# First attention of a two-block transformer: values in column halves, scores four pairs ahead, output weights by contraction tile

## The chip, the cores and the metric

One core of a Trainium2 chip runs the whole program in one launch. The metric is device time in microseconds (us). Engines: TensorE (PE) multiplies 128x128 stationary tiles with moving tiles; VectorE (DVE), ScalarE (ACT) and GpSimd (POOL) work element by element; DMA queues bring weights from memory. Products land in PSUM, in eight banks of 128 partitions by 512 floats. Each engine works through its own queue in order.

## The reference

256 tokens of 1024 features go through two blocks in float32. Block 1 is a gated-linear-attention layer (GLA), an MLP, the sliding-window attention that is edited here, and a second MLP. Block 2 is a mixer of two attentions with gates, an MLP and a gated embedding product. The edited attention, cut to what is computed:

```python
q = (h @ w_q).reshape(B, NB, BLOCK, SWA_KV_HEADS, SWA_GROUP, SWA_HEAD_DIM)   # 16 heads of 64, 2 key heads
s = einsum('bnqhgd,bnkhd->bnhgqk', q, kb) * SWA_HEAD_DIM ** -0.5             # blocks of 128 queries, 256 keys
s = where(mask, s + bias, NEG)
m = maximum(max(s, -1), sink)
p = exp(s - m)
p = p / (sum(p, -1) + exp(sink - m))
o = einsum('bnhgqk,bnkhd->bnqhgd', p, vb)
x = x + o.reshape(B, T, 1024) @ w_out
```

## The kernel before

Activations are kept transposed, features on partitions and the 256 tokens along the free axis. Every float32 weight tile is split on the chip into a high and a low part, so that one product becomes three matmuls (high by high, high by low, low by high; `mmA`, lines 271 to 276). Weights come in chunks of 1 MB (128 x 2048) by DMA; `Weights.pump` (line 64) splits half a chunk: a CAST on ACT (`wh`, L80) and a subtraction on DVE (`wl`, L81). `take` hands out the next chunk. A pump stands after each piece of matmul work, and the order of the written code is the order in each engine's queue; nothing reorders it.

`pair` multiplies one chunk, which is two outputs of 128 features over all eight contraction tiles, and yields in the middle, so that other work can be put between its halves (`Fill`). `late_two` does the same for two chunks whose input is still being made, with the last contraction tiles last.

The attention works on eight pairs of heads, f = 0 to 7. For each: `swa_scores` (S: four matmuls, then on DVE bias and maximum, L851, and small operations to L857; on ACT four exponentials, L864, in place in `s`), `swa_T` (six transposes of `s`, copied to `pt` by ACT, L874), `swa_values` (O: `pt` is stationary, and the values `vs` with a column of ones move, so that column 64 is the row sum; DVE adds the sink's term, takes the reciprocal and multiplies into `ot`, L887 to L890), `swa_oT` (OT: transposes of `ot`, split to `oT_h` by ACT and `oT_l` by DVE, L904 and L905), `swa_out` (the pair's share of the output product, for the first four outputs). Scores run two pairs ahead; the projection's third and fourth chunk (q of outputs 4 to 7) fill the first rounds. Outputs 4 to 7 are two whole chunks, `o12` and `o13`, at the end, with the residual additions (`residual`, L388, and L371, L376 for the next MLP's input `xs`) between them. Then the MLP's first product, named m1u, begins with the first six contraction tiles of four outputs.

`Banks` gives out the eight banks of PSUM in the order in which they came free. The same scheme of residuals, with all eight outputs by contraction tile, stands at the end of the GLA layer (`oa`), ahead of the MLP product m0u.

## Time and profile before

| | us |
|---|---|
| median of three runs (lowest, highest) | 1015.9 (1014.09, 1018.38) |
| profiled execution, and its span | 1012.64, 1010.9 |
| PE busy | 987.6 (98%) |
| PE weight loads | 887.5 (88%) |
| DVE busy | 656.3 (65%) |
| ACT busy | 572.6 (57%) |
| POOL busy | 214.1 (21%) |
| the stage that is edited, 328.46 to 392.03 | 63.57 |

Busy time is a share over stages with different limits. The start of a matmul is recorded, its end is modelled, so durations of successive matmuls overlap, and the distance of two starts tells the pace. A number in brackets at a line's end is the idle time of that engine ahead of it, with what ended it.

### The profile page before, as it was taken

How to read it: one execution, taken by the hardware profiler on the slowest of the kernel's cores; microseconds unless marked ns; L12 is line 12 of the kernel's file. 1: busy time of each engine (PE TensorE's matmuls, PEld its weight loads, DVE VectorE, ACT ScalarE, POOL GpSimd, SP SyncE). 2: the span in 40 equal slices, each digit the busy share in tenths (PEclk: the TensorE clock that was granted, in tenths of full speed). 3: DMA queues.
4: the chain of work that ended last, by engine and by line, in shares of the span. 5: the costliest groups of instructions: out<-in, count | busy, mean ns of one | idle time of the engine just before them, and what ended most of it. 6: DMA issues, size and time to landing. Idle time of an engine off the chain costs nothing.

```text
span 1010.9 us, 16329 instructions
## 1 busy us (share of the span) xinstructions
PE 987.6 (98%) x6540; PEld 887.5 (88%) x6540; DVE 656.3 (65%) x996; ACT 572.6 (57%) x983; POOL 214.1 (21%) x244
## 2 busy tenths in 40 slices
PE   7999999999999999999999999998999999999996
PEld 6879988888889889888888889898999988888896
DVE  5856678875555766787555537776466688755555
ACT  5734458874344665787454444365555588744343
POOL 3203123330001002333011216202212233300001
PEclk9999999999999999999999999999999999999998
DMA  7543535655557214565555633635355456555521
GB/s 265 180 165 128 181 115 204 219 197 193 195 196 239 95 62 145 190 233 205 200 175 178 221 125 123 220 114 171 121 187 189 167 173 243 174 201 190 195 84 42
DMA packets 26395, 174.47 MB, mean 173 GB/s; under 512 B 3284, under 2 KB 3576, under 8 KB 6224
## 3 DMA queue, kind: packets, MB, share of 16 engines
q1 hardware_dynamic: 24336, 168.11, 47.9%
q0 software_dynamic: 1696, 5.21, 1.8%
q8 instruction: 51, 0.84, 0.3%
q14 instruction: 24, 0.20, 0.1%
q10 hardware_dynamic: 288, 0.12, 0.0%
HBM read 172.32 MB, written 1.11 MB: 172 GB/s over the span
## 4 chain that ended last, share of the span: by engine, by line
PE 82%; DVE 8%; issue 4%; ACT 3%; POOL 2%; DMA 0%; POOLq 0%; DVEq 0%; ACTq 0%
PE m2u L280 6%; PE m1d L280 6%; PE m1u L280 6%; PE m2d L280 6%; PE m0d L280 6%; PE m0u L280 6%; PE m1u L281 3%; PE m2u L281 3%; PE m0d L281 3%; PE m2d L281 3%; PE m1d L281 3%; PE m0u L281 3%; DVE wl L81 2%; PE g L274 1%; PE g L276 1%
## 5 line engine op out<-in xcount | busy, mean ns | idle before, releaser
L81 DVE TENSOR_TENSOR wl<-raw,wh 128x1024 fp32r<-128x1024 f32 x316 | 387.6, 1248 | 126.4 <-ACT wh L80 121.0
L80 ACT CAST wh<-raw 128x1024 fp32r<-128x1024 f32 x316 | 321.6, 1047 | 84.5 <-issue 41.4
L230 POOL TENSOR_TENSOR acc<-acc,sq 128x256 f32<-128x256 f32 x52 | 39.5, 765 | 362.8 <-ACT sq L229 362.1
L720 POOL TENSOR_TENSOR us<-s,us 128x256 fp32r<-128x256 f32 x96 | 81.4, 848 | 161.9 <-ACT us L719 161.9
L280 PE MATMUL m0u<-xs,wh 128*128 128x512 f32 x256 | 89.7, 396 | 0.9 <-DVE xs L376 0.9
L280 PE MATMUL m2u<-xs,wh 128*128 128x512 f32 x256 | 89.2, 395 | 0.0
L280 PE MATMUL m1u<-xs,wh 128*128 128x512 f32 x256 | 89.1, 394 | 0.0
L280 PE MATMUL m0d<-us,wh 128*128 128x512 f32 x256 | 88.8, 394 | 0.0
L280 PE MATMUL m1d<-us,wh 128*128 128x512 f32 x256 | 88.8, 394 | 0.0
L280 PE MATMUL m2d<-us,wh 128*128 128x512 f32 x256 | 88.8, 394 | 0.0
L371 ACT ACTIVATE xs<-x,gains 128x256 fp32r<-128x256 f32 x40 | 19.0, 504 | 94.7 <-DVE x L770 72.7
L281 PE MATMUL m0u<-xs,wl 128*128 128x256 f32 x256 | 71.0, 277 | 0.0
L281 PE MATMUL m2u<-xs,wl 128*128 128x256 f32 x256 | 71.0, 277 | 0.0
L281 PE MATMUL m1u<-xs,wl 128*128 128x256 f32 x256 | 71.0, 277 | 0.0
L281 PE MATMUL m0d<-us,wl 128*128 128x256 f32 x256 | 70.9, 277 | 0.0
L281 PE MATMUL m2d<-us,wl 128*128 128x256 f32 x256 | 70.9, 277 | 0.0
L281 PE MATMUL m1d<-us,wl 128*128 128x256 f32 x256 | 70.9, 277 | 0.0
L280 PEld LDWEIGHTS m0u<-xs,wh 128*128 128x128 f32 x256 | 48.0, 188 | 12.8 <-DVE xs L376 1.8
L280 PEld LDWEIGHTS m1d<-us,wh 128*128 128x128 f32 x256 | 48.0, 188 | 11.1
L280 PEld LDWEIGHTS m2d<-us,wh 128*128 128x128 f32 x256 | 48.0, 188 | 11.1
L280 PEld LDWEIGHTS m2u<-xs,wh 128*128 128x128 f32 x256 | 48.0, 188 | 11.1
L280 PEld LDWEIGHTS m0d<-us,wh 128*128 128x128 f32 x256 | 48.0, 188 | 11.1
(387 smaller groups left out, 2503.8 us busy)
## 6 DMA issues: line engine op xcount, KB each, us to landing
raw<-in_w_up SPq DMA_DIRECT2D x48, 1024.0 KB, 4.8
raw<-in_w_dn SPq DMA_DIRECT2D x48, 1024.0 KB, 4.8
raw<-in_w_oa SPq DMA_DIRECT2D x8, 1024.0 KB, 4.8
raw<-in_w_g SPq DMA_DIRECT2D x8, 1024.0 KB, 5.0
raw<-in_w_o SPq DMA_DIRECT2D x6, 1024.0 KB, 5.0
raw<-in_w_v SPq DMA_DIRECT2D x4, 1024.0 KB, 5.6
raw<-in_w_gate SPq DMA_DIRECT2D x4, 1024.0 KB, 4.8
raw<-in_w_q SPq DMA_DIRECT2D x4, 1024.0 KB, 4.9
```

Of the source, the lines that this page charges most:

```text
L80: nc.scalar.copy(h[:, sl], t[:, sl])
L81: nc.vector.tensor_tensor(l[:, sl], t[:, sl], h[:, sl].bitcast(F32), ALU.subtract)
L230: eng.tensor_tensor(acc, acc, sq, ALU.add)
L274: mm(ps, wh, xh, start=first, stop=False, skip_group_check=True)
L276: mm(ps, wl, xh, start=False, stop=last, skip_group_check=True)
L280: mm(ps, w[0], xs[2][:, k].rearrange("p s t -> p (s t)"), start=first, stop=False, skip_group_check=True)
L281: mm(ps[:, :T], w[1], xs[0][:, k, :], start=False, stop=last, skip_group_check=True)
L371: nc.scalar.activation(self.xs[0][:, k, :], x[:, k, :], AF.Copy, scale=self.gain(k))
L720: nc.gpsimd.tensor_tensor(us[1][:, o, :], s, us[0][:, o, :].bitcast(F32), ALU.subtract)
```

## The change

The change is in this one attention, and in what orders its weights.

- Weights come as q0, keys and values, q1, q2, q3, then the output weights packed in four chunks of two contraction tiles by eight outputs. `late_two` works on q0 and keys/values together; q1 is third.
- In the stage the subtraction `wl` of a pump is held back until the next pump or `take` (`W.lag`, `settle`). Pumps stand only in every second round.
- Scores run four pairs ahead, with five buffers `s`; the exponentials also sum their rows (`accum_out`). `swa_divide` divides `s` before the transposes: on DVE, from the third pair on the second head's half on GpSimd.
- `swa_values` has `vs` (64 columns, no ones) as the stationary tile and `pt` moving, for the two heads in two column halves of the array; its output is already transposed, so `ot` and `swa_oT` are gone.
- `swa_out` adds a pair's share to all eight outputs, in four banks, from the third round on. The products `o12` and `o13` at the end are gone; residuals follow each second output of the last pair.

The diff, without three hunks of set-up and with long removed blocks cut:

```diff
@@ -77,8 +78,11 @@
...
             sl = slice(q * CH // 2, (q + 1) * CH // 2)
+            self.settle()
             nc.scalar.copy(h[:, sl], t[:, sl])
-            nc.vector.tensor_tensor(l[:, sl], t[:, sl], h[:, sl].bitcast(F32), ALU.subtract)
+            self.owed = lambda e=self.low: e.tensor_tensor(l[:, sl], t[:, sl], h[:, sl].bitcast(F32), ALU.subtract)
+            if not self.lag:
+                self.settle()
             self.part = (h, l, t, 1)
@@ -86,10 +90,18 @@
...
+    def settle(self):
+        if self.owed:
+            self.owed()
+            self.owed = None
     def take(self):
...
             self.pump()
+        if i == self.n_split - 1:
+            self.settle()
         self.cur += 1
@@ -158,8 +170,7 @@
...
     add("w_up0"), add("w_dn0")
-    add("w_q1", [0, 1]), add("w_kv"), add("w_q1", [2, 3])
-    add("w_o1k"), add("w_o1")
+    add("w_q1", [0]), add("w_kv"), add("w_q1", [1, 2, 3]), add("w_o1")
     add("w_up1"), add("w_dn1")
@@ -293,36 +305,36 @@
...
-    def pair(xs, name, evac, own=False):
+    def pair(xs, name, evac, own=False, pumps=(1, 2)):
...
         pair_part(ps, w, xs, 0, range(NK))
-        W.pump()
+        W.pump(pumps[0])
         yield
...
             B.done(ps)
-        W.pump(2)
+        W.pump(pumps[1])
         yield
-    def late_two(xs, name, late=6, mid=None):
-        ws, pss = [], []
+    def late_two(xs, name, late=6, mid=None, second=None):
+        ws, pss, xss = [], [], (xs, second or xs)
         for i in range(2):
...
             for o in range(2):
-                pair_part(pss[i], ws[i], xs, o, range(late))
+                pair_part(pss[i], ws[i], xss[i], o, range(late))
                 W.pump()
         for o in range(2):
-            pair_part(pss[0], ws[0], xs, o, range(late, NK))
+            pair_part(pss[0], ws[0], xss[0], o, range(late, NK))
         W.done(ws[0])
...
         for o in range(2):
-            pair_part(pss[1], ws[1], xs, o, range(late, NK))
+            pair_part(pss[1], ws[1], xss[1], o, range(late, NK))
         W.done(ws[1])
@@ -790,13 +802,15 @@
...
         split_x(xk, k, gcol(G_KV, k))
-    p0, p1, r_nat = late_two(xs, "q1", late=7, mid=lambda: norm_stats("n1", acc))
+    p0, ps_kv, r_nat = late_two(xs, "q1", late=7, mid=lambda: norm_stats("n1", acc), second=xk)
     w = W.take()
-    ps_kv = B.get("kv")
-    pair_part(ps_kv, w, xk, 0, range(NK))
+    p1 = B.get("q11")
+    pair_part(p1, w, xs, 0, range(NK))
     rb = norm_bcast(r_nat, "n1")
-    pair_part(ps_kv, w, xk, 1, range(NK))
+    W.pump()
+    pair_part(p1, w, xs, 1, range(NK))
     W.done(w)
+    W.lag = True
     qT = sp.tile([P, 8, 2, P], F32, name="qT")
@@ -817,10 +831,10 @@
...
             )
-    vs = sp.tile([P, 2, 2, 65], F32, name="vs")
-    nc.gpsimd.memset(vs[:, :, :, 64:65], 1.0)
+    vs = sp.tile([P, 2, 2, 64], F32, name="vs")
     vT = sp.tile([P, T], F32, name="vT")
     nc.scalar.copy(vT, ps_kv[:, T:])
+    B.done(p0, ps_kv)
@@ -828,32 +842,36 @@
...
             nc.scalar.activation(
-                vs[:, t, :, 0:64], ps[:, t * P : (t + 1) * P].rearrange("p (k d) -> p k d", k=2), AF.Copy,
+                vs[:, t], ps[:, t * P : (t + 1) * P].rearrange("p (k d) -> p k d", k=2), AF.Copy,
                 scale=r_nat[:, t : t + 1],
...
         B.done(ps)
-    q_evac(1)(p1)
-    B.done(p0, ps_kv, p1)
-    W.pump(2)
     oT = (shifted(sp, 8, "oT_h", by=24), shifted(sp, 8, "oT_l", by=0))
-    s_of, st_of, pt_of, ot_of = {}, {}, {}, {}
+    s_of, st_of, pt_of = {}, {}, {}
     def swa_scores(f):
-        s = s_of[f] = sp.tile([P, 2, 384], F32, tag="s", name=f"s{f}", bufs=3)
-        st = st_of[f] = sp.tile([P, 16], F32, tag="st", name=f"st{f}", bufs=4)
+        s = s_of[f] = sp.tile([P, 2, 384], F32, tag="s", name=f"s{f}", bufs=5)
+        st = st_of[f] = sp.tile([P, 16], F32, tag="st", name=f"st{f}", bufs=6)
         kv = f // 4
+        pss = [B.get(f"S{f}{j}") for j in range(2)]
+        for t, (lo, hi) in enumerate(((0, P), (P, 384))):
+            for j in range(2):
+                p0 = 64 * j
+                mm(
+                    pss[j][:, lo:hi], qT[p0 : p0 + 64, f, t, :], kT2[p0 : p0 + 64, kv, 0 : hi - lo],
+                    start=True, stop=True,
+                )
         for j in range(2):
-            h, p0 = 2 * f + j, 64 * j
-            ps = B.get(f"S{f}{j}")
-            mm(ps[:, 0:P], qT[p0 : p0 + 64, f, 0, :], kT2[p0 : p0 + 64, kv, 0:P], start=True, stop=True)
-            mm(ps[:, P:384], qT[p0 : p0 + 64, f, 1, :], kT2[p0 : p0 + 64, kv, :], start=True, stop=True)
+            h = 2 * f + j
             for n, (lo, hi, b) in enumerate(((0, P, biasS[:, h, P:T]), (P, 384, biasS[:, h, :]))):
                 nc.vector.tensor_tensor_reduce(
-                    s[:, j, lo:hi], ps[:, lo:hi], b, 1.0, sinks[:, h : h + 1], ALU.add, ALU.max,
+                    s[:, j, lo:hi], pss[j][:, lo:hi], b, 1.0, sinks[:, h : h + 1], ALU.add, ALU.max,
                     st[:, 2 * j + n : 2 * j + n + 1],
                 )
-            B.done(ps)
-        nc.vector.tensor_scalar(st[:, 4:8], st[:, 0:4], -1.0, None, ALU.mult)
+            B.done(pss[j])
+        nc.vector.tensor_tensor(st[:, 4:8], nhalf[:, 12:16], st[:, 0:4], ALU.mult)
         nc.vector.tensor_tensor(
@@ -861,11 +879,24 @@
...
                 c = 2 * j + n
-                nc.scalar.activation(s[:, j, lo:hi], s[:, j, lo:hi], AF.Exp, bias=st[:, 4 + c : 5 + c])
+                nc.scalar.activation(
+                    s[:, j, lo:hi], s[:, j, lo:hi], AF.Exp, bias=st[:, 4 + c : 5 + c], accum_out=st[:, 8 + c : 9 + c]
+                )
         nc.scalar.activation(st[:, 12:16], st[:, 12:16], AF.Exp)
+    def swa_divide(f):
+        s, st = s_of[f], st_of.pop(f)
+        nc.vector.tensor_tensor(st[:, 8:12], st[:, 8:12], st[:, 12:16], ALU.add)
+        nc.vector.reciprocal(st[:, 8:12], st[:, 8:12])
+        for j in range(2):
+            eng = nc.vector if f < 2 or j == 0 else nc.gpsimd
+            for n, (lo, hi) in enumerate(((0, P), (P, 384))):
+                c = 8 + 2 * j + n
+                eng.tensor_scalar(s[:, j, lo:hi], s[:, j, lo:hi], st[:, c : c + 1], None, ALU.mult)
     def swa_T(f):
-        s, st = s_of.pop(f), st_of[f]
+        s = s_of.pop(f)
         pt = pt_of[f] = sp.tile([P, 2, 3, P], F32, tag="pt", name=f"pt{f}", bufs=2)
@@ -875,29 +906,15 @@
...
     def swa_values(f):
-        kv, pt, st = f // 4, pt_of.pop(f), st_of.pop(f)
+        kv, pt = f // 4, pt_of.pop(f)
         ps = B.get(f"O{f}")
-        vv = [vs[:, t, kv, :] for t in range(2)]
-        po = ps[:, :260].rearrange("p (j t d) -> p j t d", j=2, t=2)
...
+        for t, (c0, b0, b1) in enumerate(((0, 0, 2), (P, 2, 3))):
+            for j in range(2):
+                mm(
+                    ps[64 * j : 64 * j + 64, c0:T], vs[:, t, kv, :], pt[:, j, b0:b1, :],
+                    start=(t == 0), stop=(t == 1), skip_group_check=True,
+                )
         src = rev(ps[:, :T].rearrange("p (t i) -> p t i", t=2))
@@ -905,72 +922,57 @@
...
-    okw = {}
-    def swa_out(f, accs):
-        if f % 4 == 0:
+    okw, accs = {}, []
+    def swa_out(f, after=None):
+        if f % 2 == 0:
             okw[0] = W.take()
-        for o in range(4):
+        if not accs:
+            accs.extend(B.get(f"o1{p}") for p in range(4))
+        for o in range(8):
             mmA(
-                accs[o // 2][:, (o % 2) * T : (o % 2 + 1) * T], tileA(okw[0], (f % 4) * 4 + o), colx(oT, f),
+                accs[o // 2][:, (o % 2) * T : (o % 2 + 1) * T], tileA(okw[0], (f % 2) * 8 + o), colx(oT, f),
                 first=(f == 0 and o % 2 == 0), last=(f == 7),
             )
-        if f % 4 == 3:
+            if after and o % 2:
+                after(o // 2)
+        if f % 2 == 1:
             W.done(okw[0])
-    W.ahead = 2
-    F = Fill(pair(xs, "q12", q_evac(2)), pair(xs, "q13", q_evac(3)))
-    F.run(1)
+    F = Fill(pair(xs, "q12", q_evac(2), pumps=(1, 1)), pair(xs, "q13", q_evac(3), pumps=(0, 0)))
+    W.pump()
     swa_scores(0)
     swa_v()
+    q_evac(1)(p1)
+    B.done(p1)
     F.run(1)
...
     F.run(1)
+    swa_divide(0)
+    swa_scores(2)
     swa_T(0)
-    accs = None
+    swa_divide(1)
+    swa_scores(3)
     for f in range(8):
-        if f > 0:
-            F.run(1)
...
+        F.run(1)
         if f + 1 < 8:
             swa_T(f + 1)
+        if f % 2:
+            W.pump()
         if f + 2 < 8:
-            swa_scores(f + 2)
-        if f == 0:
-            F.run(1)
+            swa_divide(f + 2)
         swa_values(f)
-        if f >= 1:
-            swa_oT(f - 1)
...
+        if f + 4 < 8:
+            swa_scores(f + 4)
+        if f >= 2:
+            swa_out(f - 2)
+    W.lag = False
+    W.settle()
     nxt = next_x(G_MLP1, by=0)
-    swa_oT(7)
-    swa_out(6, accs)
+    swa_out(6)
     W.pump()
-    w0 = W.take()
-    p0 = B.get("o12")
...
+    swa_out(7, lambda p: residual(accs[p], p, nxt, more=(p < 3)))
     W.pump(2)
```

What the written order gives on the engines, at three places. First DVE, where the projection's third chunk (`q`) is evacuated into `qT`; `s`, `st`, `S` are scores, their statistics and banks, `wl` the low part of a weight chunk. Before:

```order
L857 TENSOR_TENSOR st_3384<-st_3384,sinks 128x4
L805 SCALAR_TENSOR_TENSOR qT<-q_3332,n_rb 128x4x128
L81 TENSOR_TENSOR wl_3358<-raw_3070,wh_3357 128x1024
L887 TENSOR_TENSOR st_3265<-O_3431,st_3265 128x4
L888 RECIPROCAL st_3265<-st_3265 128x4
L890 TENSOR_TENSOR ot_3440<-O_3431,st_3265 128x2x2x64
L851 ISA s_3453,st_3454<-S_3455,biasS,sinks 128x128
```

and of the change:

```order
L819 SCALAR_TENSOR_TENSOR qT<-q_3262,n_rb 128x4x128
L83 TENSOR_TENSOR wl_3288<-raw_3071,wh_3287 128x1024
L890 TENSOR_TENSOR st_3238<-st_3238 128x4
L891 RECIPROCAL st_3238<-st_3238 128x4
L896 TENSOR_SCALAR s_3237<-s_3237,st_3238 128x128
L896 TENSOR_SCALAR s_3237<-s_3237,st_3238 128x256
L896 TENSOR_SCALAR s_3237<-s_3237,st_3238 128x128
L896 TENSOR_SCALAR s_3237<-s_3237,st_3238 128x256
L869 ISA s_3345,st_3346<-S_3347,biasS,sinks 128x128
```

The held-back subtraction and the division of pair 0, `s` by `st`, now stand between `qT` and the next pair's reduction (ISA); the add, reciprocal and multiplication of O that stood there are gone.

Second ACT in a middle round: `pt` copies, the cast into `oT_h`, the exponentials of `s`. Before:

```order
L874 COPY pt_3442<-T_3443 128x384
L874 COPY pt_3442<-T_3448 128x384
L864 ACTIVATE s_3453<-s_3453,st_3454 128x128
L864 ACTIVATE s_3453<-s_3453,st_3454 128x256
L864 ACTIVATE s_3453<-s_3453,st_3454 128x128
L864 ACTIVATE s_3453<-s_3453,st_3454 128x256
L865 ACTIVATE st_3454<-st_3454 128x4
L904 CAST oT_h<-OT_3483 128x256
L874 COPY pt_3488<-T_3489 128x384
```

and of the change:

```order
L905 COPY pt_3425<-T_3426 128x384
L905 COPY pt_3425<-T_3431 128x384
L921 CAST oT_h<-O_3442 128x256
L882 ACTIVATE s_3449,st_3450<-s_3449,st_3450 128x128
L882 ACTIVATE s_3449,st_3450<-s_3449,st_3450 128x256
L882 ACTIVATE s_3449,st_3450<-s_3449,st_3450 128x128
L882 ACTIVATE s_3449,st_3450<-s_3449,st_3450 128x256
L885 ACTIVATE st_3450<-st_3450 128x4
L905 COPY pt_3493<-T_3494 128x384
L905 COPY pt_3493<-T_3499 128x384
L82 CAST wh_3504<-raw_3162 128x1024
L921 CAST oT_h<-O_3514 128x256
```

The cast into `oT_h` follows the copies of the next pair and now reads the product O itself; with a pump in a round, a CAST of weights (`wh`) stands ahead of it. The exponentials also write into `st`.

Third DVE at the end of the stage, with the residuals (`x`) and the next MLP's input (`xs`). Before:

```order
L905 TENSOR_TENSOR oT_l<-OT_3807,oT_h 128x256
L81 TENSOR_TENSOR wl_3825<-raw_3429,wh_3824 128x1024 x2
L388 TENSOR_TENSOR x<-x,o1k_3534 128x512
L388 TENSOR_TENSOR x<-x,o1k_3535 128x512
L376 SCALAR_TENSOR_TENSOR xs<-x,gains,xs 128x256 x4
L388 TENSOR_TENSOR x<-x,o_3828 128x512
L376 SCALAR_TENSOR_TENSOR xs<-x,gains,xs 128x256 x2
L81 TENSOR_TENSOR wl_3950<-raw_3658,wh_3949 128x1024 x2
L388 TENSOR_TENSOR x<-x,o_3924 128x512
L376 SCALAR_TENSOR_TENSOR xs<-x,gains,xs 128x256 x2
L81 TENSOR_TENSOR wl_3993<-raw_3763,wh_3992 128x1024 x2
```

and of the change:

```order
L922 TENSOR_TENSOR oT_l<-O_3828,oT_h 128x256
L83 TENSOR_TENSOR wl_3742<-raw_3235,wh_3741 128x1024
L83 TENSOR_TENSOR wl_3887<-raw_3337,wh_3886 128x1024
L400 TENSOR_TENSOR x<-x,o_3583 128x512
L400 TENSOR_TENSOR x<-x,o_3584 128x512
L388 SCALAR_TENSOR_TENSOR xs<-x,gains,xs 128x256 x2
L400 TENSOR_TENSOR x<-x,o_3585 128x512
L388 SCALAR_TENSOR_TENSOR xs<-x,gains,xs 128x256 x2
L400 TENSOR_TENSOR x<-x,o_3586 128x512
L388 SCALAR_TENSOR_TENSOR xs<-x,gains,xs 128x256 x4
L83 TENSOR_TENSOR wl_3887<-raw_3337,wh_3886 128x1024
```

Before, two subtractions of m1u's first chunk stand ahead of the first residual addition, and two each for the next chunks between and behind the last ones; after the change one half of that chunk is ahead of all four additions and the other half behind the last four `xs`.

## Rows read from the trace of the kernel before

**Rows 1.** the page's chain that ended last, share of the span by engine

```profile
PE 82%; DVE 8%; issue 4%; ACT 3%; POOL 2%; DMA 0%; POOLq 0%; DVEq 0%; ACTq 0%
```

**Rows 2.** the stage: us, busy PE PEld DVE ACT POOL, PEclk, DMA, GB/s

```profile
328.46:392.03 63.57, 61.98 (x516) 55.99 (x515) 42.71 (x138) 38.29 (x92) 3.30 (x5) 1.00 0.26 89
```

**Rows 3.** PE timeline, one round: start, us, engine, line, operation, tile, count

```profile
356.20 0.50 PE L848 MATMUL S<-kT,qT 64*128 64x128 f32 x4
...
357.06 0.44 PE L883 MATMUL O<-vs,pt 128*128 128x65 f32 x2
...
358.23 0.39 PE L885 MATMUL O<-vs,pt 128*128 128x65 f32 x2
...
358.60 0.36 PE L274 MATMUL o1k<-oT_h,wh 128*128 128x256 f32 x1
...
360.09 0.82 PE L873 MATMUL T<-ident,s 128*128 128x128 f32 x6
360.84 0.50 PE L848 MATMUL S<-kT,qT 64*128 64x128 f32 x4
```

**Rows 4.** PE timeline, block 2's product in column halves

```profile
716.65 1.09 PE L1309 MATMUL OB<-ptb,vb 128*64 128x128 f32 x16
```

**Rows 5.** PE timeline, a T that waits; in brackets idle time and releaser

```profile
350.10 1.53 PE L873 MATMUL T<-ident,s 128*128 128x128 f32 x6 [0.99 <-ACT s L864]
```

**Rows 6.** timeline of ACT and DVE at the stage's start

```profile
325.84 0.37 ACT L266 COPY n_rb<-n_pb 128x256 f32<-128x256 f32 x1 [2.27 <-PE n_pb L253]
...
328.66 1.76 DVE L816 TENSOR_TENSOR kT<-kv,n_rb 64x256 f32<-64x256 f32 x4 [1.73 <-PE kv L276]
330.46 0.69 DVE L805 SCALAR_TENSOR_TENSOR qT<-q,n_rb 128x512 f32<-128x512 f32 x1
...
330.52 0.37 ACT L823 COPY vT<-kv 128x256 f32<-128x256 f32 x1 [4.30 <-DVE kT L816]
```

**Rows 7.** ACT timeline, one round; the last two lines are of block 2

```profile
364.48 1.50 ACT L864 ACTIVATE s<-s,st 128x128 f32<-128x128 f32 x4 [2.10 <-DVE st L856]
...
365.98 0.34 ACT L904 CAST oT_h<-OT 128x256 fp32r<-128x256 f32 x1
...
367.18 0.84 ACT L874 COPY pt<-T 128x384 f32<-128x384 f32 x2
...
699.00 0.18 ACT L1284 ACTIVATION_READ_ACCUMULATOR prB<-prB,stb 128x1 f32 x1
699.09 1.03 ACT L80 CAST wh<-raw 128x1024 fp32r<-128x1024 f32 x1
```

**Rows 8.** DVE timeline, rounds of the stage; the last line is of block 2

```profile
347.43 0.18 DVE L888 RECIPROCAL st<-st 128x4 f32<-128x4 f32 x1
...
356.07 0.42 DVE L905 TENSOR_TENSOR oT_l<-OT,oT_h 128x256 fp32r<-128x256 f32 x1 [0.97 <-ACT oT_h L904]
...
361.66 1.23 DVE L81 TENSOR_TENSOR wl<-raw,wh 128x1024 fp32r<-128x1024 f32 x1 [0.52 <-ACT wh L80]
362.81 0.35 DVE L851 CUSTOM_DVE_ANT_0 s<-S,biasS,sinks 128x128 f32<-128x128 f32 x1
...
669.28 0.62 DVE L1202 TENSOR_SCALAR pa<-pa,sta 128x256 f32<-128x256 f32 x2
```

**Rows 9.** DVE timeline at the end of the GLA layer

```profile
128.24 0.69 DVE L388 TENSOR_TENSOR x<-x,oa 128x512 f32<-128x512 f32 x1 [0.71 <-PE oa L276]
...
135.37 5.11 DVE L81 TENSOR_TENSOR wl<-raw,wh 128x1024 fp32r<-128x1024 f32 x4
```

**Rows 10.** windows of the first 28 steps of m1u and of m0u

```profile
392.03:401.75 9.72, 9.72 (x58) 8.56 (x57) 8.00 (x10) 6.31 (x10) 1.97 (x3) 1.00 0.40 120
...
130.84:142.39 11.55, 10.69 (x58) 8.57 (x57) 9.64 (x11) 6.88 (x12) 4.27 (x6) 1.00 0.27 94
```

**Rows 11.** windows in block 2 where the clock falls

```profile
706.00:710.00 4.00, 2.60 (x18) 2.06 (x18) 0.13 (x1) 1.17 (x2) 1.55 (x1) 0.70 0.73 242
710.00:714.00 4.00, 4.00 (x35) 3.78 (x34) 1.83 (x8) 2.09 (x5) 1.13 (x1) 0.88 0.08 31
```

More of the change, by code (lines that the diff above doesn't have):

```diff
@@ L48, in __init__ @@
         self.part, self.ahead = None, self.BUFS
+        self.lag, self.low, self.owed = False, tc.nc.vector, None
         self.loaded, self.split, self.live = {}, {}, set()
@@ L189, in stack_kernel @@
     nc.vector.memset(nhalf, -0.5)
+    nc.vector.memset(nhalf[:, 12:16], -1.0)
     def gcol(which, k):
@@ L877, in swa_values @@
     def swa_values(f):
-        kv, pt, st = f // 4, pt_of.pop(f), st_of.pop(f)
+        kv, pt = f // 4, pt_of.pop(f)
         ps = B.get(f"O{f}")
-        vv = [vs[:, t, kv, :] for t in range(2)]
-        po = ps[:, :260].rearrange("p (j t d) -> p j t d", j=2, t=2)
-        for j in range(2):
-            mm(po[:, j, 0, :], pt[:, j, 0, :], vv[0], start=True, stop=True)
-            mm(po[:, j, 1, :], pt[:, j, 1, :], vv[0], start=True, stop=False)
-            mm(po[:, j, 1, :], pt[:, j, 2, :], vv[1], start=False, stop=True)
-        rs_ = st[:, 8:12].rearrange("p (j t) -> p j t", j=2)
-        nc.vector.tensor_tensor(rs_, po[:, :, :, 64], st[:, 12:16].rearrange("p (j t) -> p j t", j=2), ALU.add)
-        nc.vector.reciprocal(rs_, rs_)
-        ot = ot_of[f] = sp.tile([P, 2, 2, 64], F32, tag="ot", name=f"ot{f}", bufs=2)
-        nc.vector.tensor_tensor(
-            ot.rearrange("p t j d -> p j t d"), po[:, :, :, 0:64],
-            rs_.unsqueeze(3).to_broadcast([P, 2, 2, 64]), ALU.mult,
-        )
-        B.done(ps)
-    def swa_oT(f):
-        ot = ot_of.pop(f)
-        ps = B.get(f"OT{f}")
-        for t in range(2):
-            nc.tensor.transpose(ps[:, t * P : (t + 1) * P], ot[:, t].rearrange("p j d -> p (j d)"), ident)
+        for t, (c0, b0, b1) in enumerate(((0, 0, 2), (P, 2, 3))):
[4 more added lines that the diff above has]
+                )
         src = rev(ps[:, :T].rearrange("p (t i) -> p t i", t=2))
@@ L928, in stack_kernel @@
     F.run(1)
+    swa_divide(0)
+    swa_scores(2)
     swa_T(0)
-    accs = None
+    swa_divide(1)
+    swa_scores(3)
     for f in range(8):
-        if f > 0:
-            F.run(1)
-        if f == 5:
-            W.ahead = W.BUFS
-        if f >= 3:
-            accs = accs or [B.get(f"o1k{p}") for p in range(2)]
-            swa_out(f - 3, accs)
+        F.run(1)
         if f + 1 < 8:
             swa_T(f + 1)
+        if f % 2:
+            W.pump()
         if f + 2 < 8:
-            swa_scores(f + 2)
-        if f == 0:
-            F.run(1)
+            swa_divide(f + 2)
         swa_values(f)
-        if f >= 1:
-            swa_oT(f - 1)
-        if f < 7:
-            W.pump()
-    swa_out(5, accs)
+        if f + 4 < 8:
[4 more added lines that the diff above has]
+    W.settle()
     nxt = next_x(G_MLP1, by=0)
-    swa_oT(7)
-    swa_out(6, accs)
+    swa_out(6)
     W.pump()
-    w0 = W.take()
-    p0 = B.get("o12")
-    for o in range(2):
-        pair_part(p0, w0, oT, o, range(7))
-        W.pump()
-    swa_out(7, accs)
-    for p in range(2):
-        residual(accs[p], p, nxt, more=(p == 0))
-    for o in range(2):
-        pair_part(p0, w0, oT, o, [7])
-    residual(p0, 2, nxt)
-    W.done(w0)
-    w0 = W.take()
-    p1 = B.get("o13")
-    for o in range(2):
-        pair_part(p1, w0, oT, o, range(8))
-        W.pump()
-    W.done(w0)
-    residual(p1, 3, nxt)
+    swa_out(7, lambda p: residual(accs[p], p, nxt, more=(p < 3)))
     W.pump(2)
@@ L1590, in _inputs @@
     m["w_q1"] = _pack_a(d["b_w_q"][0])
-    m["w_o1k"] = _pack_k(d["b_w_out"][0][:, :512], 4)
-    m["w_o1"] = _pack_a(d["b_w_out"][0][:, 512:])
+    m["w_o1"] = _pack_k(d["b_w_out"][0], 2)
     m["sinks"] = np.ascontiguousarray(d["b_sinks"][0])
```

## The prediction

> **What bounds the kernel now.** I read the chain of waits first: TensorE (PE) holds 82% of the chain that ended last, VectorE (DVE) 8%, ScalarE (ACT) 3%, and no DMA stands in it [rows 1]. So the kernel is TensorE's instruction stream plus the places where that stream waits, and the edit can win only what it takes out of the stream, and loses whatever it makes the stream wait for. The table of windows then gives the stage that is edited, from the second half of the projection q of outputs 2 and 3 to the first matmul of the next MLP (named m1u): 63.57 us, of which TensorE is busy 61.98, DVE 42.71, ACT 38.29, GpSimd 3.30, with the clock at its upper level, 1.00 [rows 2]. DVE and ACT are each idle a third of the time, but they hand work to each other, and that is where I look after the PE timeline.
>
> **What TensorE is spared.** A steady round before, read start to start, is scores S 0.86, values O and their transposes OT together 1.54, twelve output matmuls 1.49, T 0.75 [rows 3]. The new values product is written as two column halves of 64, and OT goes. Before has no such product in this stage; the nearest is block 2's OB, eight matmuls in column halves over 128 columns, sixteen records in 1.09 us [rows 4]. The new O moves 384 columns for each half where OB moves 512, three quarters of it: 0.82, an estimate from that row. Its ends: 1.54, if nothing overlaps, and 0.70, a little under half of that. So a round loses 1.54 - 0.82 = 0.72, eight rounds 5.7 us (0 to 6.7 by the two ends). The output matmuls number the same, 8 x 24, only in another order; scores and T are the same work.
> The first two records of O, behind the 64-row tiles of S, are recorded at 0.44, its last two at 0.39 [rows 3]: 0.05 for the switch. The Trainium skill's "TensorEngine Tiling (Array Packing)", section Tiling Modes, says that a change of tiling mode drains TensorE, and the new round has one change more (into the halves and out of them): by the rule and that row 8 x 0.05 = 0.4 us back, by OB's row, which holds its own changes, nothing.
> Before also waits: TensorE idles 0.99 ahead of one T, for ACT's exponentials, and that T itself is stretched to 1.53 against 0.82 of a free one [rows 3, 5]; three T's are so stretched, and two output groups a little: some 3.5 us in all. If the scores four pairs ahead take all of that away, TensorE alone would need 63.57 - 5.7 - 3.5 = 54.4 us, and m1u would start at 382.8 rather than 392.03: **9.2 us is the most the stage can win.** Three things are charged against it.
>
> **(1) The start, +1.85 us.** Both qT and kT need the normalising factor n_rb, which ACT copies at 325.84 [rows 6], and kT opens the scores. Right behind that copy the written order now has a pump, ahead of the second half of the third product: a CAST of 1.03 on ACT [rows 7] and, ahead of qT and kT on DVE, one wl of 1.23 [rows 8] (the first group of order rows shows how DVE's queue is filled ahead of the scores later in the stage). CAST 326.12 to 327.17, wl to 328.35, qT to 328.95 (0.69 by its row, some 0.08 of it overlapping), four kT to 330.7 (1.76), vT, which ACT in the row starts as the fourth kT ends, to 331.1 [rows 6]. S, the transposes of vT and q's next half follow one another on TensorE: that half starts at 331.35, and without the wait at 328.46 + 0.86 for S + 0.19 for the two transposes (OT has 0.15) = 329.5. Bounds: 0, if DVE is ahead of it, and 2.4.
>
> **(2) The DVE and ACT ping-pong, +6.2 us.** From the end of q's outputs 4 and 5, at 331.35 + 2 x 2.9 (24 matmuls each, twice the 1.49 of rows 3 less its start) + 0.86 for S and 0.1 to the DVE = 338.15 on this clock, DVE has ahead of it qT 0.6, a wl 1.15, the new divide of pair 0, the score reduce of pair 2, the divide of pair 1, the reduce of pair 3. The reduce and its small operations, from its first row to the start of the exponentials, take 364.48 - 362.81 = 1.67 [rows 7, 8]. The divide isn't there before. It is an add and a reciprocal of 0.18 each, and for each head one of 128 and one of 256 columns; two like the latter took 0.62 in block 2 [rows 8]. That is 0.36 + 2 x (0.16 + 0.31) = 1.3, less some overlap of successive starts: 1.25; its ends are 0.9 and 1.6. The sum to the exponentials of pair 3 is 0.6 + 1.15 + 1.25 + 1.75 + 1.25 + 1.67 = 7.7.
> Then the two engines alternate, since each is in order: the second group of order rows shows ACT's queue, exponentials, two pt, oT_h, and then again exponentials that wait for DVE's reduce, which is queued behind oT_l, which waits for oT_h. A turn is exponentials 1.50 and, new, four accumulator reads (0.18 recorded, 0.09 to the start of the next instruction in block 2), 1.85 in all; two pt 0.74; oT_h 0.40 with its hand-over; oT_l 0.34; reduce 1.67 [rows 7, 8]: 5.0 us. Where a pump stands in it, its CAST is 0.95 more (1.03 recorded). Turns for pairs 3, 4, 5 are 5.0 + 5.95 + 5.0, and the last exponentials and the first copy pt 2.3: 338.15 + 7.7 + 15.95 + 2.3 = 364.1. That copy frees a bank: with four of the eight banks held by the output accumulators from the third round, the second score matmul of pair 7 has to wait for it. TensorE's own work up to that point is five T 3.75, four O 3.28, five S 4.3, two halves of q 5.84 and one output group 2.88, 20.1 us from 337.9, so it would be there at 358.0, and is late by some 6.2. From the third pair on the second head's divide is GpSimd's; its five instructions in the stage took 3.30 [rows 2], so two take some 1.3, which lies beside ACT's 3.0 of a turn. Bounds: 0, if the turns overlap, and 9.
> After it nothing is late until the end: m1u starts at 382.8 + 1.85 + 6.2 = 390.9, 1.1 earlier than before.
>
> **(3) The end, +5.1 us.** Before, the residual adds of the last outputs are spread: 24 output matmuls without a dependence on the last pair and then whole weight products lie between them, and the first chunk of m1u is split in full ahead of them. After, as the third group of order rows shows, one wl of m1u's first chunk stands ahead of the four adds and the eight products xs, the other half behind them all. The twin of it in this kernel is the end of the GLA layer: four adds and eight xs there too, from the second add at 128.24 to the wl behind the last xs at 135.37 without a pause to speak of, 7.13, and the first add 0.69 more: 7.8 of DVE work [rows 9]. New: the last output group starts at 390.9 - 2.9 = 388.0 (24 matmuls, twice the 1.49 of rows 3), its first add is 1.0 later, 389.0; + 7.85 = 396.85; the wl 1.25 more, 398.1. m1u's first output half fits into the wait, its second half takes six steps of 9.72/28 = 0.347 [rows 10], and is done at 400.2. Before, the same point is 392.03 + 12 x 0.347 = 396.2. **The net of the whole change is +4.0 us.** Chunk 58 and the rest of m1u then follow as before.
>
> **The sum.** -9.2 + 1.85 + 6.2 + 5.15 = +4.0, against the profiled execution's 1012.64 (span 1010.9 and 1.7 around it): 1016.6. The median of the runs shown is 1015.9, 3.3 above the profiled one, so the same difference puts the changed kernel at **1019.9**. A measurement of this kernel tells about 0.5% from no change, 5.1 us, so this is a "same" that leans to slower.
>
> **Rivals.**
> *The clock falls at the end (+5.7, 1021.6).* In (3) TensorE idles some 5 us in two pieces. In 706 to 710 TensorE was busy 2.60 of 4.00 us, and the granted clock came out at 0.70 there and at 0.88 in the next 4 us [rows 11]: part of both ran at the lower level, 1.2 GHz, and 4.00 x (0.30 + 0.12) = 1.7 us of full-speed work was lost. The same at m1u's start adds 1.7. It decides once TensorE stands as idle there as in that stretch, 1.40 us of 4; against it, the GLA end, with 0.86 of idle, stayed at 1.00 [rows 10].
> The Trainium skill's "TensorE: Matmul & The Clock Gate", part 1, What's actually happening, says that "the default state is throttled, and activity releases the throttle"; the 0.70 agrees, and the 1.00 shows that a short wait leaves it released.
> *The ping-pong is covered (-2.2, 1013.7).* If DVE and ACT overlap their turns (oT_h ready early, reduce ahead of it), (2) is nothing. For it: both have a third of the stage to spare [rows 2]; against it: each turn's hand-overs stand in the queues in that order.
> *Covered, and the end costs no more than at the GLA layer (-5.8, 1010.1).* There the 28 steps took 11.55, here 9.72: 1.83 us of wait [rows 10], as its first chunk was split in full. Against it: here half a chunk is behind.
> That the new O isn't sped up at all (its upper end, 1.54) gives 5.7 more in TensorE work, but the ping-pong hides most of it.
>
> **Chances.** My forecast 0.48 (alone from +1 to +6.5: 1016.9 to 1022.4), clock 0.15, covered 0.22, covered with a short end 0.11, anything else 0.04. The range takes in all but the far ends: 1009.8 to 1023.5. Faster by over 0.5%: most of the last rival and a little of the covered one, 0.12. Slower by over 0.5%: two thirds of the clock's, a seventh of the forecast's and the rest, 0.20. Same: 0.68.
>
> **What would show it.** O's records of a round start to start 0.7 to 0.95; q's third pair 1.5 to 2.4 us later than 329.5, with vT and kT named as releaser; waits of TensorE at the first T and at pair 7's scores, released by pt or by DVE; ACT's exponentials idle on st for 1.5 us and more; m1u waiting 4 to 6 us in its first twelve steps, for wl. The prediction is wrong if m1u starts before 388 (the ping-pong is covered), or if its first twelve steps take under 6 us.

## The result, and the profile after

The changed kernel takes 1024.83 us (median of 8 runs, 1020.62 to 1027.97) against 1015.68 (8 runs, 1012.48 to 1018.38): ratio 1.0098, interval 1.0074 to 1.0122. It is slower by about 9 us; 1019.9 was forecast. The profiled executions differ by the same 9.0 (span 1019.9 and 1010.9).

Where these lie is read from the starts of matmuls in the two traces, cut at marks that both programs have (a step of m1u is one weight tile, two matmuls):

| stretch | before | after | difference | forecast |
|---|---|---|---|---|
| start to the broadcast of n_rb | 325.43 | 326.49 | +1.06 | 0 |
| broadcast to m1u's first matmul | 66.60 | 65.93 | -0.67 | -1.1 |
| m1u's first 28 steps | 9.72 | 17.94 | +8.22 | +5.1 |
| the rest | | | +0.4 | 0 |

The first row is no part of the change: in the GLA layer, some 270 us ahead, the granted clock of this one execution fell to 0.64 from 58 to 62, and in before it did not (of the versions below, it fell there in e3, e6, e7 and e11 too). The chain, by engine [rows 1]:

```profile
PE 86%; DVE 7%; ACT 3%; issue 2%; POOL 1%; DMA 1%; SPq 0%; POOLq 0%; DVEq 0%; ACTq 0%
```

The attention's part of TensorE, from its timeline [rows 3 to 6]:

```profile
330.55 1.34 PE L862 MATMUL S<-kT,qT 64*128 64x128 f32 x8 [0.96 <-DVE kT L830]
332.21 0.44 PE L842 MATMUL vs<-ident,vT 128*128 128x128 f32 x2 [0.32 <-ACT vT L836]
...
347.41 0.87 PE L914 MATMUL O<-pt,vs 128*64 128x256 f32 x8
348.21 0.93 PE L862 MATMUL S<-kT,qT 64*128 64x128 f32 x8
```

O takes 0.80 start to start (0.82 forecast, 1.54 with OT before). S waits for kT and then vs for vT, at the places of part (1). All of TensorE's waits from the stage's start to the end of m1u's first steps, in the view of waits (engine, what waited, for what: us in total, times, longest):

```profile
PE m1u L292 <- ACT wh L82: 2.4, 1, 2.4
PE S L862 <- ACT pt L905: 1.9, 1, 1.9
PE T L904 <- DVE s L896: 1.9, 2, 1.7
PE m1u L292 <- DVE xs L388: 1.1, 3, 0.5
PE S L862 <- DVE kT L830: 1.0, 1, 1.0
PE m1u L293 <- DVE wl L83: 0.6, 1, 0.6
PE T L904 <- POOL s L896: 0.5, 1, 0.5
PE vs L842 <- ACT vT L836: 0.3, 1, 0.3
```

The second and the third row are the ping-pong of part (2): pair 7's scores, and the first T with 1.7 of the 1.9. Three rows are m1u's. Its windows, with the columns of [rows 2], answer to [rows 10]:

```profile
392.42:396.00 3.58, 2.57 (x12) 1.46 (x10) 3.58 (x7) 3.01 (x9) 2.62 (x4) 1.00 0.00 0
396.00:400.00 4.00, 1.41 (x3) 0.59 (x3) 2.27 (x4) 3.57 (x8) 3.17 (x4) 0.85 0.00 0
400.00:404.00 4.00, 3.46 (x11) 2.97 (x12) 4.00 (x6) 2.91 (x4) 0.00 (x0) 0.50 0.63 197
404.00:408.00 4.00, 4.00 (x21) 3.50 (x20) 2.33 (x2) 2.00 (x2) 0.00 (x0) 0.80 1.01 385
```

TensorE is busy 1.41 of 4 us from 396, and then the clock stands at 0.50, its lower level, while TensorE has work. Seven steps from 400.93 to 405.40 take 0.64 each instead of 0.347: 2.0 us, some 2.3 with the step ahead of them, so 5.9 of the 8.2 are waiting. What is waited for, on ACT, DVE and GpSimd [rows 9]:

```profile
395.82 0.42 ACT L241 ACTIVATE sq<-x 128x256 f32<-128x256 f32 x1 [0.57 <-POOL acc L242]
...
397.77 0.42 ACT L241 ACTIVATE sq<-x 128x256 f32<-128x256 f32 x1 [0.43 <-POOL acc L242]
398.10 4.82 ACT L82 CAST wh<-raw 128x1024 fp32r<-128x1024 f32 x5
```
```profile
390.46 1.41 DVE L400 TENSOR_TENSOR x<-x,o 128x512 f32<-128x512 f32 x2 [3.56 <-PE o L288]
...
396.67 1.35 DVE L388 SCALAR_TENSOR_TENSOR xs<-x,gains,xs 128x256 fp32r<-128x256 f32 x2 [0.60 <-ACT xs L383]
399.15 2.47 DVE L83 TENSOR_TENSOR wl<-raw,wh 128x1024 fp32r<-128x1024 f32 x2 [1.14 <-ACT wh L82]
```
```profile
393.95 5.45 POOL L242 TENSOR_TENSOR acc<-acc,sq 128x256 f32<-128x256 f32 x6 [0.43 <-ACT sq L241]
```

The second half of m1u's first chunk is cast at 398.10 and subtracted at 399.15, 8.69 us behind the first addition, against 7.85 in the forecast. The CAST stands behind the squares of the residuals, and the squares wait for GpSimd, which adds them up one by one. DVE itself stands idle for 0.60 and 1.14 us in this stretch: ACT's queue, not DVE's, ends last.

### The profile page after: what moved, and what is told of

It reads as the page before. It is cut to its first block, busy times and chain, and to the rows that moved or that the text cites. A ratio compares the mean times of both kernels' runs of the same rounds, so it can differ in the third digit from the quotient of the medians.

```text
span 1019.9 us, 16297 instructions
## 1 busy us (share of the span) xinstructions
PE 987.2 (97%) x6492; PEld 882.2 (86%) x6492; DVE 658.9 (65%) x1009; ACT 575.3 (56%) x1015; POOL 224.5 (22%) x255
## 4 chain that ended last, share of the span: by engine, by line
PE 86%; DVE 7%; ACT 3%; issue 2%; POOL 1%; DMA 1%; SPq 0%; POOLq 0%; DVEq 0%; ACTq 0%
PE m2u L292 6%; PE m1d L292 6%; PE m0d L292 6%; PE m2d L292 6%; PE m1u L292 6%; PE m0u L292 6%; PE m1u L293 3%; PE m2u L293 3%; PE m2d L293 3%; PE m0d L293 3%; PE m1d L293 3%; PE m0u L293 3%; DVE wl L83 2%; PE o L286 1%; PE g L286 1%
## 5 line engine op out<-in xcount | busy, mean ns | idle before, releaser
L292 PE MATMUL m1u<-xs,wh 128*128 128x512 f32 x256 | 92.2, 404 | 3.6 <-ACT wh L82 2.4
L292 PEld LDWEIGHTS m1u<-xs,wh 128*128 128x128 f32 x256 | 49.2, 192 | 16.1 <-ACT wh L82 2.8
```

The costliest lines, as they stand in the source:

```text
L292: mm(ps, w[0], xs[2][:, k].rearrange("p s t -> p (s t)"), start=first, stop=False, skip_group_check=True)
```

## Experiments

All runs, with the stage from the broadcast of n_rb to m1u, m1u's first 28 steps, and the mean granted clock in each, from the windows of the profiled executions. The ratio is to the kernel before on the same chip; it is not the quotient of the two medians.

| run | stage, clock | 28 steps, clock | ratio (interval) |
|---|---|---|---|
| before | 66.60, 1.00 | 9.72, 1.00 | 1 |
| changed | 65.93, 1.00 | 17.94, 0.81 | 1.0098 (1.0074 to 1.0122) |
| e1_chunk_whole | 67.57, 0.97 | 13.58, 1.00 | 1.0027 (1.0005 to 1.0049) |
| e2_warm | 67.55, 0.97 | 15.69, 1.00 | 1.0056 (1.0034 to 1.0078) |
| e3_start | 64.60, 0.97 | 17.14, 0.90 | 1.0058 (1.0032 to 1.0085) |
| e4_out_later | 67.05, 1.00 | 17.30, 0.90 | 1.0069 (1.0041 to 1.0097) |
| e5_divide_first | 64.75, 0.97 | 17.56, 0.81 | 1.0103 (1.0080 to 1.0126) |
| e6_low_on_pool | 66.22, 1.00 | 17.86, 0.81 | 1.0094 (1.0072 to 1.0116) |
| e7_halves_alone | 99.49, 0.79 | 9.89, 1.00 | 1.0337 (1.0318 to 1.0356) |
| e9_squares | 69.12, 0.95 | 12.57, 1.00 | 1.0048 (1.0018 to 1.0077) |
| e10_by_output | 69.07, 0.95 | 11.72, 1.00 | 1.0041 (1.0022 to 1.0060) |
| e8_best | 65.64, 0.97 | 10.57, 1.00 | 1.0010 (0.9989 to 1.0030) |
| e11_low_behind | 63.07, 1.00 | 17.63, 0.81 | 1.0074 (1.0052 to 1.0095) |
| e12_best_low | 60.77, 1.00 | 10.57, 1.00 | 0.9984 (0.9972 to 0.9997) |

A stage at 0.95 to 0.97 lost 1.5 us and more to the clock, mostly behind the wait at pair 7's scores; whether it does differs between executions. The code up to there is the same in the changed kernel and in e1, and so is the wait, 1.9 us; the changed kernel's windows, and e1's:

```profile
362.00:366.00 4.00, 1.99 (x18) 1.30 (x16) 3.19 (x13) 2.95 (x12) 1.18 (x2) 1.00 0.00 0
366.00:370.00 4.00, 4.00 (x35) 3.57 (x32) 2.87 (x15) 1.91 (x7) 0.74 (x2) 1.00 0.00 0
```
```profile
362.00:366.00 4.00, 2.06 (x9) 1.22 (x10) 2.28 (x7) 3.80 (x13) 1.55 (x2) 0.81 0.00 0
366.00:370.00 4.00, 4.00 (x28) 4.00 (x29) 2.85 (x15) 1.96 (x9) 1.52 (x2) 0.77 0.00 0
```

TensorE is idle for some 2 us of the 4 in both, and one keeps its clock.

**The end.**

```diff
     swa_out(6)
-    W.pump()
+    W.pump(2)
     swa_out(7, lambda p: residual(accs[p], p, nxt, more=(p < 3)))
```

> The changed kernel with one more pump ahead of the last pair's output matmuls, so that both halves of m1u's first weight chunk are split before the residual additions, as at the GLA layer's end. Theory (the late half chunk makes TensorE idle for 5.9 us in m1u's first 28 steps, and the idling costs the clock, 2.3 us more): the 28 steps fall from 17.95 to about 11.5 us, the clock stays at 1.00 there, the time falls by 6.4 to about 1018.4, ratio to before 1.003. Rival (the residuals' squares, which GpSimd adds up, hold ACT and so xs): the steps stay at 15 us or more, the time falls by 2 us at most. Rival (only the clock matters, not the chunk): 28 steps at 15.6.

13.58: the steps fell by 4.4, less than the 6.4 of the theory and more than the rivals', with the clock at 1.00, and the ratio by 0.7%. So the late half chunk is the larger part, but the GLA layer isn't the twin I took it for. The rest of the wait has moved to the second chunk, whose CAST also stands behind the squares (398.49).

```diff
+                    if name == "m1" and o == 0:
+                        ps = B.get("warm")
+                        for _ in range(24):
+                            mm(ps[:, :T], tileA(ws[p], 0)[0], xs[0][:, 0, :], start=True, stop=True)
+                        B.done(ps)
```

> The changed kernel with 24 matmuls of 256 columns that write to an unused bank, behind the first six steps of m1u, where TensorE idles for 2.7 us; nothing reads their result. Theory (half of the junction's loss beyond the wait is the clock): they fit into the idle time, the granted clock stays at 1.00 to 0.9 instead of 0.5 from 399 to 405, the first 28 steps fall from 17.95 to about 15.7 by themselves (the added matmuls within), time about 1022.6. Rival (the slow steps after the wait come from a late operand, not from the clock): the steps are as long as before or longer, 1024.8 to 1027.

15.69 with the 24 matmuls within, as the theory had it, and the clock at 1.00 where it was 0.50; the window that answers to that of 396 to 400 after:

```profile
396.00:400.00 4.00, 3.74 (x28) 3.37 (x27) 2.26 (x4) 3.53 (x7) 3.35 (x5) 1.00 0.00 0
```

Work that nobody needs made the kernel 2 us shorter there: the slow steps were the clock's, and 2.3 is its price.

```diff
...
-            sq = npool.tile([P, T], F32, tag="sq", name="sq")
+            sq = sq_of[0]()
...
+    sq_of[0] = lambda: sp.tile([P, 2, 384], F32, tag="s", name="sq", bufs=5)[:, 0, :T]
...
```

> The kernel of the run with the whole first chunk split early, with five buffers instead of two for the squares of the last residuals, so that ACT need not wait until GpSimd has added one up. Theory: ACT's two waits for GpSimd (0.56 and 0.44 us) are gone, the CAST of m1u's second chunk comes 1.0 us earlier, and m1u's first 28 steps take 12.6 instead of 13.6 us. Rival (the products xs on DVE beside GpSimd set it): within 0.3 us of 13.6.

12.57: as the theory had it, 1.0 us less than 13.58. The two squares' buffers are what tied ACT to GpSimd.

```diff
...
-    swa_out(6)
-    W.pump()
-    swa_out(7, lambda p: residual(accs[p], p, nxt, more=(p < 3)))
+    W.pump(2)
+    for p in range(4):
+        for f in (6, 7):
+            swa_out(f, range(2 * p, 2 * p + 2))
+        residual(accs[p], p, nxt, more=(p < 3))
```

> The changed kernel with only its end altered: m1u's first chunk split in full ahead of the residuals, and the last two pairs' output matmuls output by output with each residual behind its own, as at the GLA layer's end. Theory (the end is a chain of DVE and ACT work that begins with the first addition): the first addition comes 2.1 us earlier, m1u's first 28 steps take 11.4 us, like the GLA layer's, with no loss of clock; 1018, ratio 1.002 to 1.003. Rival (the second chunk, still split behind the residuals, is what is waited for): 13 us or more, no better than with the chunk alone, ratio 1.004.

The steps are 11.72, as in the GLA layer (11.55 there), with the first addition 4.1 us ahead of m1u instead of 2.0. The ratio 1.0041 is above the 1.002 to 1.003 that I expected, but its interval holds them; in the one execution that was profiled the stage was at 0.95.

**The start and the turns.**

```diff
     rb = norm_bcast(r_nat, "n1")
-    W.pump()
     pair_part(p1, w, xs, 1, range(NK))
...
     nc.scalar.copy(vT, ps_kv[:, T:])
+    W.pump()
```

> The changed kernel with the pump behind the normalising factor's copy moved behind the copy vT, so that no CAST and no wl stand ahead of qT and kT. Theory: TensorE's waits for kT and vT, 1.8 us, are gone and nothing takes their place, as the next DVE work starts from the end of the third q product: m1u starts 1.8 us earlier behind the third product, time about 1023.0. Rival (the subtraction moved comes back in DVE's queue later): the wait at the first T grows by 1 to 1.2 us, and the time falls by 0.7 or less.

TensorE's waits for kT and vT are gone, the wait at the first T is still 1.7, so the subtraction doesn't come back there, and the stage is 1.3 shorter, between the two, with the clock lost after the wait ahead of the first T (0.64 from 345 to 349), which the changed kernel's profile didn't have.

```diff
-    F.run(1)
     swa_divide(0)
+    F.run(1)
     swa_scores(2)
```

> The changed kernel with the first pair's division put ahead of the evacuation of q's third product (DVE is idle for 1.19 us there), so that it no longer stands between that evacuation and the reduction. Theory (DVE and ACT set the pace from there on): TensorE's wait of 1.7 us at the first T is gone, and since the later turns begin 1.2 us earlier, m1u starts 1.2 us earlier behind the third product. Rival (TensorE's own work sets the pace and the wait only moves): the wait at the last scores grows by as much, m1u within 0.4 us of where it was.

The stage is 1.18 shorter, as the theory had it, and the wait at the first T is gone: T starts at 339.12, right behind the scores. A wait of 0.8 for the division now stands at the fourth T, where the changed kernel waits 0.2, and the clock falls there (0.57 from 354 to 358). It doesn't lengthen the stage: TensorE comes later to pair 7's scores and waits 0.8 there instead of 1.9, for a copy that DVE and ACT's turns bring 1.18 earlier. The ratio shows nothing of it.

```diff
-        if f >= 2:
-            swa_out(f - 2)
+        if f >= 3:
+            swa_out(f - 3)
+    swa_out(5)
```

> The changed kernel with the output matmuls three rounds behind instead of two, so that the four accumulators take their banks only after the last scores. Theory (DVE and ACT hand work to each other and set the pace; the missing bank is only where it shows): TensorE's wait of 1.9 us at the last scores is gone, and 2 to 3 us of waiting appear at the fifth T or ahead of it, where the first output group stood; from the first T to m1u's start the same within 0.7 us. Rival (the banks themselves cost it): no new wait, m1u 2 us earlier, time about 1022.6.

The wait of 1.9 is gone and others stand in its place (0.7 more for T from DVE, 0.5 from GpSimd, 0.8 for oT_l, 0.6 for pt): from the first T to m1u 51.66 against 50.64. That is 1.0 longer, more than the 0.7 that the theory allowed, but with the rival's 2 us excluded: the bank was not the cause.

```diff
-    W.lag = True
+    W.lag, W.low = True, nc.gpsimd
...
```

> The changed kernel with the held-back subtractions of the stage (wl) on GpSimd instead of DVE. Theory (DVE is one of the two engines that set the pace): three subtractions of 1.15 us leave the turns, and m1u starts 1.2 to 2.4 us earlier. Rival (GpSimd, at about 3.4 us for one by four times its 0.85 for 256 columns, is now late for the divisions and slows DVE beside it): TensorE waits for GpSimd at T by 2 us and more in all, m1u 1 to 3 us later.

Neither: 0.3 longer. The DVE timeline and GpSimd's show why:

```profile
333.86 2.34 DVE L874 TENSOR_TENSOR st<-nhalf,st 128x4 f32<-128x4 f32 x1
...
340.61 1.48 DVE L890 TENSOR_TENSOR st<-st 128x4 f32<-128x4 f32 x1
```
```profile
333.78 2.39 POOL L83 TENSOR_TENSOR wl<-raw,wh 128x1024 fp32r<-128x1024 f32 x1 [9.19 <-ACT wh L82]
339.71 2.35 POOL L83 TENSOR_TENSOR wl<-raw,wh 128x1024 fp32r<-128x1024 f32 x1 [3.54 <-ACT wh L82]
```

A DVE operation on four columns, 0.15 to 0.16 us elsewhere, ends when GpSimd's subtraction ends. Ahead of the first T DVE waits out more than it was spared. Reductions that read PSUM kept their 0.35 and 0.48 beside GpSimd. The Trainium skill's "GPSIMD Engine Reference", section Specifications, says that the SBUF interfaces are shared with VectorE and that VectorE instructions with two SBUF inputs contend; these rows agree.

Behind the first T the turns keep their length: `oT_l` starts at 350.98, 356.92, 361.92 and 367.86 here, at 350.09, 356.03, 361.04 and 366.99 in the changed kernel. One of these in e6, and the same in the changed kernel:

```profile
356.92 0.42 DVE L922 TENSOR_TENSOR oT_l<-O,oT_h 128x256 fp32r<-128x256 f32 x1 [2.16 <-ACT oT_h L921]
```
```profile
356.03 0.42 DVE L922 TENSOR_TENSOR oT_l<-O,oT_h 128x256 fp32r<-128x256 f32 x1 [1.03 <-ACT oT_h L921]
```

Without the subtraction DVE only waits longer for ACT's oT_h. So in these turns the subtraction had stood where DVE would have idled, and the theory was wrong that it lengthens them.

```diff
...
-        swa_values(f)
+        low = swa_values(f)
         if f + 4 < 8:
             swa_scores(f + 4)
+        low()
```

(`low` is the DVE half of the split of O; ACT's oT_h stays where it was.)

> The changed kernel with one DVE instruction of each round moved: the low part oT_l behind the next scores' reduction instead of ahead of it, so that the reduction no longer waits for oT_h, which waits for ACT's exponentials. Theory (the hand-over from ACT to DVE and back in each turn sets the pace): the exponentials idle less than 0.7 us on st instead of 2.0, TensorE's wait of 1.9 us at the last scores falls under 0.5, and the stage from the broadcast of the factor to m1u takes 63.5 us (65.9 in the changed kernel); the end stays at 17 to 18. Rival (it is the bank: the copy pt is late, whatever DVE does): the wait of 1.9 us stays, 65.5 or more.

The stage takes 63.07 and the wait at pair 7's scores has left the list: the theory. ACT's exponentials still wait, about 1 us each behind the first and more than the 0.7 expected, though less than in the changed kernel, where the row reads 11.8 in the same stretch:

```profile
ACT s L882 <- DVE st L874: 8.1, 6, 3.2
```

One instruction's place in DVE's queue was worth 2.9 us of the stage.

**One part alone, on the kernel before.** Values in halves with `swa_divide` ahead of each `swa_T`, scores two pairs ahead:

```diff
...
         if f + 1 < 8:
+            swa_divide(f + 1)
             swa_T(f + 1)
...
```

> The kernel before with one part of the change alone: values in column halves, with the row sums and the division ahead of the transposes that they need; weight order, scores two pairs ahead, pumps and the end stay as before. Theory (TensorE's 0.72 a round is off the path, since division and accumulator reads lengthen the turns of DVE and ACT): TensorE's stage takes 61 to 65 us instead of 63.57 with more waits, ratio to before 0.997 to 1.002. Rival (TensorE's work decides): the stage takes 58 us, ratio 0.9945.

Both are wrong: 99.49, and 3.4% slower. The waits, and one stretch of the stage:

```profile
PE T L884 <- DVE s L876: 22.1, 7, 4.6
```
```profile
360.00:370.00 10.00, 6.68 (x30) 4.38 (x31) 3.13 (x16) 4.43 (x19) 1.55 (x2) 0.50 0.00 1
```

With the division ahead of the transposes, reduction, exponentials, division and T of one pair stand in line, and two pairs ahead leaves nothing to put beside them; TensorE idles for 3 to 4 us a round, and its clock is 0.50 in the stretch shown and 0.79 over the stage. So the four pairs ahead are not an extra of this change: with the division ahead of the transposes, two are not enough. Three pairs, and halves with the division behind the values product, were not tried.

**The version that the runs point to.** e8: the edits of e3, e5 and e9, the outputs by pairs of e10 with three pumps; e12: the same with e11's.

> All that the runs so far point to, on the changed kernel: the pump behind vT, the first division ahead of q's evacuation, the squares in five buffers, three pumps instead of one ahead of the last outputs, and the last two pairs' output matmuls taken output by output, so that the residual additions start some 2 us earlier under TensorE's work. Theory (start, DVE and ACT's turns, and the late chunk are the loss, and add up): the stage from the broadcast of the factor to m1u 62.5 to 63.5 us (65.9 in the changed kernel), m1u's first 28 steps 10.3 to 11.2 (17.95), the clock at 1.00 there; 1014 to 1015.5, ratio to before 0.997 to 1.000. Rival (the parts don't add up, as a wait removed is met again at the last scores): the stage 65 and the steps 12.5, ratio 1.004.

The end as expected (10.57), the stage not: 65.64, with the same wait of 1.9 at pair 7's scores and the clock lost behind it. That wait ends 1.8 earlier behind the broadcast than in the changed kernel, and the clock takes 1.5 of it back; the rival had it right for the stage.

> The best version so far with the same instruction moved. Theory: the wait of 1.9 us at the last scores is gone, and the 1.5 us of slow clock behind it with it; the stage falls from 65.6 to 62 us, m1u's first 28 steps stay at 10.6, ratio to before 0.996 to 0.9985. Rival (the waits go elsewhere): stage 64 or more, ratio 1.000 or more.

The stage is 60.77, below the 62 expected, with these waits left in it and in the 28 steps:

```profile
PE T L907 <- POOL s L899: 0.5, 1, 0.5
PE O L917 <- ACT pt L908: 0.4, 1, 0.4
PE m1u L295 <- DVE xs L391: 0.3, 1, 0.3
PE T L907 <- DVE s L899: 0.2, 1, 0.2
```

Up to there it is 5.0 us ahead of before (-5.8 and +0.85). The ratio is 0.9984 (medians 1012.1 and 1012.84), at the edge of what a measurement tells, and 1.1% below the changed kernel's. Its profiled execution gave the 5 us back where no edit touches the program: 3.2 in the next MLP (last section), and 1.9 behind it, where the clock fell in block 2 (0.91 from 635 to 655, 1.00 there in before).

## Why the prediction was wrong

*What TensorE is spared* held: O 0.80 for 0.82, and no switch of tiles beyond it. Of the 9.2 some 0.7 did not come, most of it in a term that was at nothing: the output matmuls number the same, but the last 72 stand 0.121 us apart and before the 54 of `o13` 0.117. Why is open.

*(1) The start*, +1.85, held: kT comes 1.03 later and the first scores take 0.8 longer (S 1.66 start to start instead of 0.86): 1.83. e3 takes the waits away.

*(2) The ping-pong*, +6.2, held in its parts too. The forecast turns were 5.0, 5.95 and 5.0; ACT's exponentials of pairs 3 to 6 start 4.99, 5.95 and 5.01 apart:

```profile
347.10 0.40 ACT L882 ACTIVATE s<-s,st 128x128 f32<-128x128 f32 x1 [0.38 <-DVE st L874]
...
352.09 0.41 ACT L882 ACTIVATE s<-s,st 128x128 f32<-128x128 f32 x1 [2.03 <-DVE st L874]
...
358.04 0.40 ACT L882 ACTIVATE s<-s,st 128x128 f32<-128x128 f32 x1 [2.03 <-DVE st L874]
...
363.05 0.40 ACT L882 ACTIVATE s<-s,st 128x128 f32<-128x128 f32 x1 [2.04 <-DVE st L874]
```

TensorE's waits at the first T, the fourth, the fifth and pair 7's scores, with what they stretch, are 1.73 + 0.35 + 0.28 + 1.03 + 0.21 + 2.42 = 6.0 from start to start. e4 and e11 show that it is the hand-over and not the bank; e6 shows that DVE's load behind the first T isn't it. What I had not seen is that it doesn't end there: in five of the other profiled versions (e1, e2, e8, e9, e10) the clock falls behind its last wait.

*(3) The end*, +5.1, is the step that failed, in its size: 8.2. The mechanism was the one named, the half chunk behind all residuals (e1). Two terms were wrong. The wait is 5.9 and not 5.1: I counted DVE's queue, but ACT's ends last, as the CAST stands behind squares that wait for GpSimd's sums (e9: 1.0); the GLA layer's end, from which I took 7.8 us, hides that because its additions come 1.4 us apart (e10 makes them so, and has its 11.7). And the clock's fall, 2.3 us, I had as a rival at 0.15 and 1.7 us, excused by the same GLA layer, whose wait was 0.86 of idle where I had worked out five (e2 is the proof). I should have compared the idle time that I forecast with the idle time in [rows 11], which it exceeded, and made the clock's fall the likelier case; not a certain one, as the changed kernel's 362 to 366 shows. 4.0 + 2.3 + 0.8, with the 0.7 of the outputs and the 0.2 by which (2) stayed short, is 7.6, the 7.55 by which the two profiled executions differ from the broadcast to m1u's 28th step. What the medians show beyond that, 9.15, has no single place here; the clock lost inside the stage in other executions is the likely part, and no run isolates it.

So the forecast "same, leaning to slower" had sign and place right, and what came was its first rival, with a larger price. "Covered" and "covered with a short end" are excluded: the waits stand in the list. (The sum of the latter is off: by its own terms it is -5.5, 1010.4, not -5.8; nothing rests on it.) The two signs of being wrong that were named did not come: m1u started at 392.42, and its first twelve steps took 11.7 us. They could not have told of an end that costs more.

## What to carry to other kernels

A saving on TensorE is worth what the engines that feed it can deliver: look at the order of the queues for instructions that wait for one another across engines in turn (here oT_h, oT_l, reduction, exponentials), and count one turn, not the busy shares. Work that stands in a turn where its engine would wait anyhow costs nothing, and moving it gains nothing (e6). When a change leaves TensorE idle for as long as a stretch of the trace after which the clock fell, count the clock's price as the likelier case: behind one and the same wait of 1.9 us it fell in five versions here and held in the changed kernel and in e6. Split or load what the next stage needs first ahead of a residual, and keep the buffers between ACT and a slow GpSimd deep enough that ACT does not wait.
